# A hybrid encoder layer on one core: where in the program the weight sums of the down projection's Strassen groups are fetched

## The chip, the cores and the metric

The kernel runs on one core of a Trainium2 chip. The metric is the device time of one execution in microseconds (us), lower is better. The kernel before takes 2408.36 us, the median of three runs (2406.69 to 2409.8).

## The reference

One layer of a bidirectional encoder, in float32, on two requests of 256 tokens with 2048 features (512 tokens together):

```python
def encoder_layer(h, ...):
    xn = rmsnorm(h, norm_mix_w)
    proj = xn @ w_in                       # neighbourhood attention + gated delta net
    ...
    h = h + mixed                          # mixed = concat(...) @ w_out
    hn = rmsnorm(h, norm_ffn_w)
    return h + (jax.nn.silu(hn @ w_gate) * (hn @ w_up)) @ w_down
```

and a last rmsnorm. This document is about the last product, `(...) @ w_down`: 5632 hidden features to 2048, for 512 tokens.

## The kernel before, in words

**Arithmetic.** A float32 matrix is split into a high part (rounded to the fast float32 format by ScalarE, line 134) and a low part (the difference, VectorE, line 135). A product of two such matrices takes two or three matmuls. Every weight tile goes through this split on its way to TensorE.

**Stages.** In order of time: the input projection with the attention and delta-net heads (to about 900 us of the trace), the output projection, then gate and up (`scaled`, about 970 to 1840 us), then the down projection (1843 us to the end).

**A block.** Gate, up and most of down are computed by `block` (lines 969 to 1031). It is one step of a Strassen-like scheme with seven products instead of eight: two tiles of output features by two halves of the tokens, from four weight quarters `w11, w21, w12, w22`. A product (`product`, line 937) is a run of k-tiles, with two matmuls for each: 8 k-tiles in gate and up, 7 in the down projection (`GROUP = 7`). The seven products run on TensorE in this order, each with its weights and its PSUM tile:

1. `w11` (tile b11) into `ps_a`
2. `second = w12 + w22` into `ps_c`
3. `first = w11 + w12` into `ps_d`
4. `w21` (tile b21), into `ps_a` again
5. `first + b22` into `ps_b`
6. `w22` (tile b22), into `ps_d` again
7. `first + b21`, into `ps_c` again

The two sums `first` and `second` are made by DMA: a plain fetch of one quarter on SP's queue (lines 976 and 977), and then an accumulating fetch of the other on POOL's queue (`plus`, line 967, issued from lines 978 and 979), which can only be issued when the plain one has landed. The tiles b11, b21 and b22 are plain fetches on SP (lines 982 to 984). So a block has five plain loads and two accumulating ones. VectorE adds b22 (line 1015) and b21 (line 1027) to `first` in place.

Products are read out by VectorE and ScalarE (lines 949 to 953, 1003, 1009, 1020, 1021). The block's result is the tile `out`. It is created after the first product (line 996) and first written after the fourth, by ScalarE's copy of line 949 called from line 1013. At the end of the block it is added into the residual `hT` (line 1152).

**The down projection.** It runs in this order: a segment of 4 tiles done plainly (`down`), beside which the seven activation tiles of group 0 are combined (`combine`); group 0 (`down_group`, 8 blocks); another plain segment, beside which group 1 is combined; group 1 (8 blocks); two plain segments and the last norm. In the trace the blocks of group 0 start at 1881.30 us and end at 2069.85, those of group 1 go from 2113.41 to 2297.43. After blocks 2 and 4 of a group, `load_act` fetches one tile of the activations of the following plain segment, on POOL's queue (line 1119).

**Buffers.** All of these share one ring of five buffers, tag `ra` (`ring`, line 1101): the temporaries of `combine`, the two sums of a block, its `out`, and `load_act`'s tiles. The tiles b11, b21, b22 have a ring of three (tag `raw`), and the split weights have three high and three low parts. In gate and up, by contrast, `first` and `second` have buffers of their own, one set for gate and one for up.

**Order.** Matmuls are kept in the program's order. All other instructions are ordered on their engine when the program is compiled, by readiness and priority. The priority of an instruction is its place in the program, and `tc.high_priority(offset=n)` moves it n places ahead. `AHEAD` is 120. The splits of the weights have this offset, and the fetches at the head of a block 3 x 120 = 360. A block has about 140 instructions. SP and POOL issue their DMAs in the order so found, and an instruction that waits holds up those behind it on its queue. An instruction that is the first to write a tile needs a free buffer of the tile's ring.

Of the kernel before, what the change touches and what calls it, by code (L numbers as in the profile page):

```python
# [8 lines left out]
F32 = mybir.dt.float32  # L9
# [9 lines left out]
P = 128  # L19
# [5 lines left out]
L = 256  # L25
# [8 lines left out]
GROUP = 7  # L34
# [8 lines left out]
AHEAD = 120  # L43
# [26 lines left out]
def hybrid_encoder(ctx: ExitStack, tc: tile.TileContext, xT, w_in, w_ba, w_out, w_gate,  # L70
# [822 lines left out]
    XC = [hp.tile([P, 7, 2, L], F32R, tag=f"xc{k}", name="xc") for k in range(8)]  # L893
    ga_cm = tc.tile_pool(name="gA", bufs=1, side="left", reuse_waits="tile")
    gA = ga_cm.__enter__()
    acc = gA.tile([P, T], F32, tag="acc", name="ssq_acc2")
    A11, S3, S1, A12, S2, S4, A22 = range(7)
    for n, i in enumerate(pairs):
        j = i % 8
# [62 lines left out]
    def ahead():  # L962
        return tc.high_priority(offset=AHEAD)

    def plus(dst, src):

        nc.gpsimd.dma_start(dst, src, accum_op=ALU.add)

    def block(w4, new_w, xc, ix, p1_pool, new_out, opened=None):


        n = len(xc)
        w11, w21, w12, w22 = w4
        with tc.high_priority(offset=3 * AHEAD):
            first, second = new_w("first"), new_w("second")
            nc.sync.dma_start(second, w12)
            nc.sync.dma_start(first, w11)
            plus(second, w22)
            plus(first, w12)
            b11, b21, b22 = [wp.tile([P, 8, P], F32, tag="raw", bufs=3, name=nm)[:, :n]  # L980
                             for nm in ("b11", "b21", "b22")]
            nc.sync.dma_start(b11, w11)
            nc.sync.dma_start(b21, w21)
            nc.sync.dma_start(b22, w22)

        def bank(pool_, tag, nm):
            return pool_.tile([P, T], F32, tag=tag, name=nm).rearrange("p (a t) -> p a t", a=2)

        pa, pb = bank(pg, "g", "ps_a"), bank(pso, "o0", "ps_b")
        pc, pd = bank(psm, "s", "ps_c"), bank(pso, "o1", "ps_d")  # L990
        with ahead():
            w = w_split(b11)
        product(pa, w, xc, ix[A11], True)
        if opened:
            opened()
        fp, out = state["fp"], new_out()
        p1 = p1_pool.tile([P, L], F32, tag="p1", name="p1")
        plus_both(p1, None, pa)
        with ahead():
            w = w_split(second)  # L1000
        product(pc, w, xc, ix[S3], True)
        p7 = fp.tile([P, 2, L], F32, tag="p7", name="p7")
        nc.scalar.copy(p7, pc)
        with ahead():
            w = w_split(first)
        product(pd, w, xc, ix[S1], True)
        if opened:
            token_rstd2()
        tt(p7, pd, p7, ALU.subtract)
        with ahead():  # L1010
            w = w_split(b21)
        product(pa, w, xc, ix[A12], False, True)
        plus_both(out[:, 0], None, pa)
        with ahead():
            tt(first, first, b22, ALU.add)
            w = w_split(first)
        product(pb, w, xc, ix[S2], True, True)
        u2 = fp.tile([P, L], F32, tag="u2", name="u2")
        plus_both(u2, p1, pb)
        tt(out[:, 3], p7[:, 0], u2, ALU.subtract)  # L1020
        tt(out[:, 3], out[:, 3], p7[:, 1], ALU.add)
        with ahead():
            w = w_split(b22)
        product(pd, w, xc, ix[S4], False, True)
        plus_both(out[:, 2], u2, pd, ALU.subtract)
        with ahead():
            tt(first, first, b21, ALU.add)
            w = w_split(first)
        product(pc, w, xc, ix[A22], False, True)
        plus_both(out[:, 1], u2, pc)  # L1030
        return out
# [18 lines left out]

    def scaled(src, f, pool, new_out, opened=None):
        w4 = (src[f, 0], src[f, 1], src[f + 1, 0], src[f + 1, 1])
        out = block(w4, lambda nm: pool.tile([P, 8, P], F32, tag=nm, name="w_" + nm), XC,
                    range(7), gA, new_out, opened)
        a = out.rearrange("p (f b) t -> p f (b t)", f=2)
        tt(a, a, state["rstd2"][:, None, :].broadcast_to([P, 2, T]), ALU.mult)
        return out
# [37 lines left out]
    fq = ctx.enter_context(tc.tile_pool(name="fq", bufs=1, side="right", reuse_waits="tile"))  # L1095
    state["fp"] = fq
    XD = [hq.tile([P, 7, 2, L], F32R, tag=f"xd{k}", name="xd") for k in range(GROUP)]

    ix = (0, 3, 4, 1, 5, 6, 2)

    def ring(shape, nm):
        return fq.tile([P] + shape, F32, tag="ra", bufs=5, name=nm)
# [21 lines left out]
    def down(s, a, beside=None, first=False, residual=False):  # L1124

        for j in range(8):
# [14 lines left out]
            if residual:  # L1141
                plus(hcol(j), s_h2[2 * j:2 * j + 2].rearrange("i p t -> p i t"))

    def down_group(g, s):

        a = state["new_sA"]()
        for j in range(8):
            out = block([w_group[g, j, i] for i in range(4)],
                        lambda nm: ring([GROUP, P], "w_" + nm), XD, ix, fq,
                        lambda: ring([4, L], "out"))  # L1150
            h4 = hcol(j).rearrange("p i t -> p (i t)")
            tt(h4, h4, out.rearrange("p a t -> p (a t)"), ALU.add)
            if j in (2, 4):
                load_act(s, a, [j // 4])
        return a
# [148 lines left out]
```

## Time and profile before

| | |
|---|---|
| median of 3 runs | 2408.36 us (2406.69 to 2409.8) |
| the profiled execution | 2404.11 us, its span 2402.3 us, mean granted clock of TensorE 0.981 |
| TensorE busy | 2309.1 us, 96% of the span |
| VectorE busy | 1793.2 us, 75% |
| ScalarE busy | 1065.9 us, 44% |
| HBM | 163 GB/s over the span |
| group 0, blocks 0 to 7 | 1881.30 to 2069.85 us |
| group 1, blocks 0 to 7 | 2113.41 to 2297.43 us |

How to read the profile. PE is TensorE, PEld its weight loads, DVE VectorE, ACT ScalarE, POOL GpSimd, SP the sync engine. `L976` is line 976 of the kernel. `w_second<-in_w_group_dram` names what is written and what it is read from; buffer numbers are left out, so all blocks carry the same names. `SPq` and `POOL` with `DMA_DIRECT2D` are the issues of DMAs; the transfer itself ends some microseconds later. In a row of the timeline the columns are the start (us from the span's start), the length, engine, line, operation, tiles, and in brackets how long the engine had been idle and what ended that. In the rows of waits: who waited for whom, us in total, times, and the longest. A wait for several things is put down to what came last, so "DVE out" beside a POOL issue can stand for a DMA. In the view by windows each pair is the busy time and the count of one engine; PEclk is the granted clock as a share of the full one.

### The profile page before, as it was taken

To read this page: it belongs to the slowest core of one execution; us is meant where nothing else is said; L and a number is where in the kernel's file an instruction comes from. 1 tells how busy PE (TensorE), PEld (TensorE's weight loads), DVE (VectorE), ACT (ScalarE), POOL (GpSimd) and SP (SyncE) were. 2 spreads that over 40 slices of the span, in tenths; PEclk is the share of its full clock that TensorE was granted. 3 is DMA by queue.
4 is the path that set the end of the run, shared out by engine and by line. 5 is a ranking of instruction groups with operands and counts; after the bars stand their busy time and mean duration, and the time that the engine had idled before them with its cause. 6 is when DMAs were issued, how large, how long until landed. Compare 5 with 4: busy or idle time off the path is not lost.

```text
span 2402.3 us, 32408 instructions
## 1 busy us (share of the span) xinstructions
PE 2309.1 (96%) x12316; PEld 1940.6 (81%) x12316; DVE 1793.2 (75%) x2698; ACT 1065.9 (44%) x1626; POOL 246.3 (10%) x350
## 2 busy tenths in 40 slices
PE   9999999999999999999999999999999978988897
PEld 7887778887877788888888888888888767777687
DVE  7644899965656438988888888888888766866666
ACT  6786332343334216544444444444445423433335
POOL 2112100011000000101010101111000010000110
PEclk9999999999999999999999999999999989999899
DMA  5335322374335536777777677777774554554572
GB/s 198 132 110 157 104 101 93 105 173 143 130 116 177 170 123 222 206 203 202 203 198 200 189 215 194 209 203 195 199 184 156 142 162 125 183 152 135 163 184 89
DMA packets 113980, 393.19 MB, mean 164 GB/s; under 512 B 14336, under 2 KB 14800, under 8 KB 112544
## 3 DMA queue, kind: packets, MB, share of 16 engines
q1 hardware_dynamic: 78416, 275.56, 33.1%
q0 software_dynamic: 35408, 115.56, 22.4%
q8 instruction: 97, 1.59, 0.3%
q14 instruction: 59, 0.48, 0.1%
HBM read 355.59 MB, written 35.47 MB: 163 GB/s over the span
## 4 chain that ended last, share of the span: by engine, by line
PE 69%; DVE 15%; DMA 7%; ACT 5%; issue 4%; SPq 0%; POOL 0%; ACTq 0%; DVEq 0%; POOLq 0%
PE ps_g L82 21%; PE ps_c L82 13%; PE ps_d L82 12%; PE ps_a L82 11%; PE ps_b L82 6%; DMA w_second<-in_w_group_dram 5%; PE ps_s L82 5%; DVE w_lo L135 4%; ACT w_hi L134 2%; DVE prod L550 2%; DVE W L552 2%; PE ps_o L82 1%; DVE cacc L339 1%; DMA w_first<-in_w_group_dram 1%; ACT E L457 1%
## 5 line engine op out<-in xcount | busy, mean ns | idle before, releaser
L82 PE MATMUL ps_g<-xhi,w_hi 128*128 128x512 f32 x896 | 362.0, 404 | 2.1 <-DVE on L427 1.4
L82 PE MATMUL ps_g<-xhi,w_lo 128*128 128x512 f32 x896 | 350.8, 392 | 2.5 <-DVE w_lo L135 2.5
L82 PE MATMUL ps_g<-xlo,w_hi 128*128 128x512 f32 x896 | 350.4, 391 | 0.6 <-DVE xlo L243 0.4
L135 DVE TENSOR_TENSOR w_lo<-w_first,w_hi 128x1024 fp32r<-128x1024 f32 (+1 forms) x180 | 214.0, 1189 | 120.9 <-ACT w_hi L134 116.9
L134 ACT ACTIVATE w_hi<-w_raw 128x1024 fp32r<-128x1024 f32 x166 | 175.0, 1056 | 272.2 <-PE ps_g L82 213.3
L135 DVE TENSOR_TENSOR w_lo<-w_raw,w_hi 128x1024 fp32r<-128x1024 f32 x166 | 202.6, 1221 | 116.1 <-ACT w_hi L134 112.7
L134 ACT ACTIVATE w_hi<-w_first 128x1024 fp32r<-128x1024 f32 (+1 forms) x180 | 185.8, 1032 | 231.2 <-PE ps_c L82 105.7
L134 ACT ACTIVATE w_hi<-b 128x1024 fp32r<-128x1024 f32 (+1 forms) x180 | 185.6, 1031 | 218.9 <-issue 123.1
L82 PE MATMUL ps_a<-xc,w_hi 128*128 128x512 f32 x704 | 251.7, 397 | 1.0
L82 PE MATMUL ps_d<-xc,w_hi 128*128 128x512 f32 x704 | 249.7, 394 | 0.0
L82 PE MATMUL ps_c<-xc,w_hi 128*128 128x512 f32 x704 | 249.7, 394 | 0.0
L135 DVE TENSOR_TENSOR w_lo<-b,w_hi 128x1024 fp32r<-128x1024 f32 (+1 forms) x180 | 213.3, 1185 | 11.6 <-ACT w_hi L134 4.6
L82 PEld LDWEIGHTS ps_g<-xhi,w_hi 128*128 128x128 f32 x896 | 168.7, 188 | 39.7 <-issue 6.6
L82 PEld LDWEIGHTS ps_g<-xhi,w_lo 128*128 128x128 f32 x896 | 168.5, 188 | 39.9 <-DVE w_lo L135 3.9
L82 PE MATMUL ps_a<-xc,w_lo 128*128 128x256 f32 x704 | 197.0, 280 | 0.0
L82 PE MATMUL ps_c<-xc,w_lo 128*128 128x256 f32 x704 | 196.9, 280 | 0.0
L82 PE MATMUL ps_d<-xc,w_lo 128*128 128x256 f32 x704 | 196.9, 280 | 0.0
L82 PEld LDWEIGHTS ps_g<-xlo,w_hi 128*128 128x128 f32 x896 | 168.8, 188 | 34.6 <-DVE xlo L243 1.8
L82 PEld LDWEIGHTS ps_a<-xc,w_hi 128*128 128x128 f32 x704 | 131.9, 187 | 36.6 <-issue 6.3
L82 PE MATMUL ps_c<-xd,w_hi 128*128 128x512 f32 x224 | 105.0, 491 | 53.9 <-ACT w_hi L134 53.9
L82 PEld LDWEIGHTS ps_c<-xc,w_hi 128*128 128x128 f32 x704 | 131.9, 187 | 30.7
L82 PEld LDWEIGHTS ps_d<-xc,w_hi 128*128 128x128 f32 x704 | 131.9, 187 | 30.7
(358 smaller groups left out, 4752.6 us busy)
## 6 DMA issues: line engine op xcount, KB each, us to landing
w_raw<-in_w_in_dram SPq DMA_DIRECT2D x110, 512.0 KB, 3.3
b<-in_w_gate_dram SPq DMA_DIRECT2D x66, 512.0 KB, 4.2
b<-in_w_up_dram SPq DMA_DIRECT2D x66, 512.0 KB, 5.5
b<-in_w_group_dram SPq DMA_DIRECT2D x48, 448.0 KB, 4.9
w_raw<-in_w_out_dram SPq DMA_DIRECT2D x32, 512.0 KB, 3.4
w_raw<-in_w_down_dram SPq DMA_DIRECT2D x32, 512.0 KB, 4.3
w_second<-in_w_gate_dram SPq DMA_DIRECT2D x22, 512.0 KB, 8.1
w_first<-in_w_gate_dram SPq DMA_DIRECT2D x22, 512.0 KB, 5.8
```

Source lines behind the costliest of these rows:

```text
L82: pin(nc.tensor.matmul(*a, **k))
L134: act(out=hi, in_=src, func=AF.Copy)
L135: tt(lo, src, r32(hi), ALU.subtract)
L339: stt(a3[:, :, lo:hi], x3[:, :, lo + o:hi + o], cw[:, ct, j:j + 1], a3[:, :, lo:hi], ALU.mult, ALU.add)
L457: pin(act(out=E[half[0], s, s:], in_=G[half[0], s:], func=AF.Exp, bias=NG[half[0], s:s + 1]))
L550: tt(pv, W[:, s0:s1, s0:c], kkq[:, c, 0, None, s0:c].broadcast_to([P, n, j]), ALU.mult)
L552: nc.vector.tensor_reduce(W[:, s0:s1, c], pv, AX.X, ALU.add)
```

## The change

The fetch of the two sums becomes a function of its own, `weight_sums`, with the same four DMAs in the same order and the same priority offset. `block` takes the two sums ready made. In gate and up, `scaled` calls `weight_sums` directly ahead of `block`, so that nothing moves there. In `down_group` the sums of block 0 are fetched ahead of the loop, and those of block j+1 inside block j: `block` calls `new_out()` after its first product, which creates `out` and then calls `group_sums(g, j + 1)`. In the program the fetches of block j+1 thus stand behind the first product of block j, ahead of the instructions that evict it, instead of at the head of block j+1.

```diff
-    def block(w4, new_w, xc, ix, p1_pool, new_out, opened=None):
-
-
-        n = len(xc)
+    def weight_sums(w4, new_w):
+
         w11, w21, w12, w22 = w4
         with tc.high_priority(offset=3 * AHEAD):
             first, second = new_w("first"), new_w("second")
...
             nc.sync.dma_start(first, w11)
             plus(second, w22)
             plus(first, w12)
+        return first, second
+
+    def block(w4, sums, xc, ix, p1_pool, new_out, opened=None):
+
+        n = len(xc)
+        first, second = sums
+        w11, w21, w12, w22 = w4
+        with tc.high_priority(offset=3 * AHEAD):
             b11, b21, b22 = [wp.tile([P, 8, P], F32, tag="raw", bufs=3, name=nm)[:, :n]
                              for nm in ("b11", "b21", "b22")]
             nc.sync.dma_start(b11, w11)
...
+    def group_sums(g, j):
+        return weight_sums([w_group[g, j, i] for i in range(4)],
+                           lambda nm: ring([GROUP, P], "w_" + nm))
+
     def down_group(g, s):
 
         a = state["new_sA"]()
+        sums = [group_sums(g, 0)]
+
+        def new_out():
+            out = ring([4, L], "out")
+            if j < 7:
+                sums.append(group_sums(g, j + 1))
+            return out
+
         for j in range(8):
-            out = block([w_group[g, j, i] for i in range(4)],
-                        lambda nm: ring([GROUP, P], "w_" + nm), XD, ix, fq,
-                        lambda: ring([4, L], "out"))
+            out = block([w_group[g, j, i] for i in range(4)], sums[j], XD, ix, fq, new_out)
             h4 = hcol(j).rearrange("p i t -> p (i t)")
             tt(h4, h4, out.rearrange("p a t -> p (a t)"), ALU.add)
```

More of the change, by code (lines that the diff above doesn't have):

```diff
@@ L1052, in scaled @@
         w4 = (src[f, 0], src[f, 1], src[f + 1, 0], src[f + 1, 1])
-        out = block(w4, lambda nm: pool.tile([P, 8, P], F32, tag=nm, name="w_" + nm), XC,
-                    range(7), gA, new_out, opened)
+        sums = weight_sums(w4, lambda nm: pool.tile([P, 8, P], F32, tag=nm, name="w_" + nm))
+        out = block(w4, sums, XC, range(7), gA, new_out, opened)
         a = out.rearrange("p (f b) t -> p f (b t)", f=2)
```

## The prediction

> **What bounds the kernel now.** I read the page first: the busy shares, the 40 slices, and the chain that ended last.
>
> ```profile
> PE 2309.1 (96%) x12316; PEld 1940.6 (81%) x12316; DVE 1793.2 (75%) x2698; ACT 1065.9 (44%) x1626; POOL 246.3 (10%) x350
> PE   9999999999999999999999999999999978988897
> PEclk9999999999999999999999999999999989999899
> PE ps_g L82 21%; PE ps_c L82 13%; PE ps_d L82 12%; PE ps_a L82 11%; PE ps_b L82 6%; DMA w_second<-in_w_group_dram 5%; PE ps_s L82 5%; DVE w_lo L135 4%; ACT w_hi L134 2%; DVE prod L550 2%; DVE W L552 2%; PE ps_o L82 1%; DVE cacc L339 1%; DMA w_first<-in_w_group_dram 1%; ACT E L457 1%
> ```
>
> TensorE is full in 31 slices, and then come the slices of the down projection's two groups with 7 and 8. The chain has one large DMA in it, the fetch of a weight sum of the groups: 5% of 2402 us is 120 us. So I asked for the sums by stretch: blocks 1 to 7 of group 0, the same of group 1, and, to compare, eight blocks of the gate and up projections, which run the same seven products over eight k-tiles instead of seven. Columns: length, then busy us (and count) of PE, weight loads, DVE, ACT and POOL, granted clock, DMA share, GB/s.
>
> ```profile
> 1902.56:2069.85 167.29, 136.63 (x688) 115.05 (x687) 108.91 (x151) 57.66 (x75) 13.38 (x17) 0.89 0.53 145
> 2131.61:2297.43 165.82, 137.16 (x688) 115.71 (x687) 108.98 (x150) 56.88 (x73) 13.43 (x18) 0.90 0.54 148
> 1301.01:1458.83 157.82, 157.60 (x903) 137.64 (x902) 135.03 (x174) 71.75 (x85) 15.98 (x20) 1.00 0.71 195
> ```
>
> A gate block takes 157.82/8 = 19.73 us with TensorE never idle and the clock at 1.00. The larger tiles should cost 8/7 of a group block, so a group block's own matmul time is 19.73 x 14/16 = 17.26 us (each k-tile is two matmuls). But a group block takes 167.29/7 = 23.90 and 165.82/7 = 23.69 us. TensorE is idle 30.66 + 28.66 = 59.3 us there, and its clock is 0.89 and 0.90. What ends the idle time (the waits of this stage: us, times, longest), and one block boundary in order of time:
>
> ```profile
> ACT w_hi L134 <- DMA w_second<-in_w_group_dram: 128.7, 15, 10.6
> PE ps_c L82 <- ACT w_hi L134: 53.9, 15, 5.2
> ...
> 1965.87 0.33 SPq L983 DMA_DIRECT2D b<-in_w_group_dram  x1
> 1966.25 0.42 SPq L976 DMA_DIRECT2D w_second<-in_w_group_dram  x1
> 1966.72 0.42 SPq L977 DMA_DIRECT2D w_first<-in_w_group_dram  x1
> 1967.24 0.38 SPq L984 DMA_DIRECT2D b<-in_w_group_dram  x1
> ...
> 1966.30 0.37 ACT L949 COPY out<-ps_a 128x256 f32<-128x256 f32 x1 [1.59 <-PE ps_a L82]
> ...
> 1972.16 0.85 POOL L967 DMA_DIRECT2D w_second<-in_w_group_dram  x1 [22.26 <-DVE out L952]
> 1973.36 0.86 POOL L967 DMA_DIRECT2D w_first<-in_w_group_dram  x1 [0.34 <-issue]
> ...
> 1973.52 0.40 PE L82 MATMUL ps_a<-xd,w_hi 128*128 128x512 f32 x1
> ...
> 1979.28 0.95 ACT L134 ACTIVATE w_hi<-w_second 128x896 fp32r<-128x896 f32 x1 [9.63 <-DMA w_second<-in_w_group_dram]
> 1980.29 0.80 PE L82 MATMUL ps_c<-xd,w_hi 128*128 128x512 f32 x1 [4.13 <-ACT w_hi L134]
> 1982.07 0.95 ACT L134 ACTIVATE w_hi<-w_first 128x896 fp32r<-128x896 f32 x1 [1.84 <-DMA w_first<-in_w_group_dram]
> ```
>
> A block starts on TensorE at 1973.52. Its second sum was fetched at 1966.25, added to by POOL's DMA at 1972.16, and split by ACT at 1979.28: 13.0 us from fetch to use. A product lasts 17.26/7 = 2.47 us, so the second product could begin at 1976.0; it begins at 1980.29. That is 4.3 us late, in 15 of 16 blocks.
>
> **Why the fetch is late.** The sums share a ring of five buffers with `out`. The fetch has a priority of 360 places ahead, yet it leaves at the moment when `out` of the block before is first written: 1966.25 against 1966.30. It is the same one block into the group, where the ring is nearly empty (the last temporary of the seven combinations is written at 1880.01, its last reader starts at 1881.56, and only the two sums of block 0 are live):
>
> ```profile
> 1880.01 0.42 DVE L1110 TENSOR_TENSOR cmd<-raw_a,cmd 128x256 f32<-128x256 f32 x1
> 1881.56 1.23 DVE L135 TENSOR_TENSOR xd<-cmd,xd 128x1024 fp32r<-128x1024 f32 x1 [1.13 <-ACT xd L134]
> ...
> 1895.33 0.37 SPq L976 DMA_DIRECT2D w_second<-in_w_group_dram  x1
> ...
> 1895.34 0.37 ACT L949 COPY out<-ps_a 128x256 f32<-128x256 f32 x1 [1.60 <-PE ps_a L82]
> 1896.95 1.09 DVE L135 TENSOR_TENSOR w_lo<-w_first,w_hi 128x896 fp32r<-128x896 f32 x1 [0.75 <-ACT w_hi L134]
> ```
>
> I read this so: buffers of a ring are given out in the order in which the program first writes the tiles, not by priority and not by which is free. `out` is first written after the fourth product (line 1013), and the next block's sums come behind it. Creation order is not what counts: `first` is created before `second`, but the rows have L976 (`second`) ahead of L977 (`first`), as the program writes them.
>
> **The change, part by part.** No instruction is added or removed. The two plain fetches (SP) and the two accumulating ones (POOL) of block j+1 are now written in the program behind block j's first product and ahead of `out`'s first write. By the reading above the ring's order becomes: sums of j+1, then `out` of j. So the sums of j+1 can leave as soon as `out` of block j-1 has its buffer and one is free. Second: `out` of j-1 is written 1973.52 - 1966.30 = 7.2 us before block j starts, which is 24.5 us before block j+1 does. It needs 13.0 us and is wanted 1.5 us into the block (one product less ACT's 0.95): some 13 us to spare, where it now lacks 4.3. First: with `out` of j-1, the sums of j and `first` of j-1 in the ring, its buffer comes when `first` of j-1 is split for the last time; that split ends at 1896.95 + 1.09 = 1898.04, 4.5 us before the next block (1902.56), so it leaves 21.8 us ahead of block j+1. From 1966.72 to 1982.07 it takes 15.4 us, and it is wanted 4 us into the block: 10 us to spare.
>
> The queues passed (issues of the whole run: KB each, median us to landing):
>
> ```profile
> b<-in_w_group_dram SPq DMA_DIRECT2D x48, 448.0 KB, 4.9
> w_second<-in_w_group_dram SPq DMA_DIRECT2D x16, 448.0 KB, 4.2
> w_second<-in_w_group_dram POOLq DMA_DIRECT2D x16, 448.0 KB, 7.2
> w_first<-in_w_up_dram POOLq DMA_DIRECT2D x22, 512.0 KB, 8.8
> ```
>
> On SP the sums now stand a block ahead of where they were, among the same five loads of 448 KB per block; SP's issues take 0.33 to 0.42 us (above). Their buffer is free by then, so they hold up b21 (1965.87) or b22 by one issue. On POOL they pass the two loads of the segment's activations per group, which are not due for blocks. Nothing new waits.
>
> The gain: blocks 1 to 7 fall to 17.26 us each. Group 0: 167.29 - 7 x 17.26 = 46.5 us; group 1: 165.82 - 120.8 = 45.0 us; together 91.5 us. Of this 59.3 is recorded idle time, and 32.2 is matmuls that run slowly behind it. The clock of 0.89 and 0.90 in the rows above says why: it drops at each wait. The Trainium skill ("TensorE: Matmul & The Clock Gate", Part 1) states that after an idle window of about 3.4 us the array runs at half clock for about as long again; that would be an estimated 1.7 us for each of 14 waits, 24 us, and a gain of 83 us instead of 91.5. The trace agrees in kind (0.89 to 0.90 against 1.00) and has 2.3 us for each.
>
> What comes late next, and its price. (1) DVE. It is the cover's thinnest part:
>
> ```profile
> 1973.52:1997.85 24.33, 19.87 (x101) 16.58 (x99) 16.12 (x22) 8.69 (x11) 2.83 (x4) 0.86 0.56 155
> 1997.85:2021.78 23.93, 19.12 (x100) 16.24 (x99) 15.07 (x21) 7.67 (x10) 1.12 (x3) 0.93 0.51 130
> 2113.41:2131.61 18.20, 17.57 (x99) 14.97 (x98) 13.42 (x19) 7.56 (x10) 0.80 (x1) 1.00 0.46 132
> ```
>
> DVE is busy 15.07 us per block, 16.12 with a load of activations, against 17.26: 87% and 93%. The gate blocks hide 135.03/157.82 = 86% without a trace of a stall. I bound it by 0 (the gate) and 0.7 us per block (10 us in 14 blocks), and take 0.2 us: 3 us, nearest to the gate. (2) Block 0 of each group. Its own sums come just in time (the last row is block 0 of group 1: 18.20 us, 0.63 idle), and now those of block 1 are fetched right behind them. Two plain loads of 448 KB at the gate's 195 GB/s are 2 x 2.35 = 4.7 us of traffic. It costs nothing if the sums of block 0 are ahead in every queue, and up to 4.7 us per group if they share: I take 1.5 each, 3 us. (3) DMA bandwidth: a group moves 148 GB/s x 23.69/17.26 = 203 GB/s afterwards, beside 195 at a share of 0.71 in the gate; no price, but it is in bound (1).
>
> **Sum.** 91.5 - 3 - 3 = 85.5 us. The profiled execution took 2404.1 us (span 2402.3 and 1.8 around it), so 2318.6; the median of the three runs is 4.3 above it, which gives 2322.9, say 2323. For the best case, the first matmuls of two products of a block that follow each other:
>
> ```profile
> 2014.50 0.39 PE L82 MATMUL ps_b<-xd,w_hi 128*128 128x512 f32 x1
> 2016.93 0.39 PE L82 MATMUL ps_d<-xd,w_hi 128*128 128x512 f32 x1
> ```
>
> No residue and products of 2016.93 - 2014.50 = 2.43 us (17.0 per block): 167.29 + 165.82 - 238 = 95, so 2313. Worst of this case: 91.5 - 10 - 9.4 = 72: 2336.
>
> **Rivals.**
> *A, the change doesn't move the fetch.* If buffers go in order of creation, `out` is still created ahead of the sums, and they leave as now, at L949: 2408. For it: in the diff `ring([4, L], "out")` does stand first. Against it: L976 ahead of L977, above. 0.07.
> *B, the loads of the block's own weights become the late ones.* If the early sums stand ahead of b21 on SP and wait for a buffer that the add into `hT` frees, b21 comes late (the add's row, in the block boundary above):
>
> ```profile
> 1974.64 1.22 DVE L1152 TENSOR_TENSOR hT<-hT,out 128x1024 f32<-128x1024 f32 x1
> ```
>
> The add ends at 1975.86, 2.3 us after the block's start. b21 leaves at start + 2.8, lands a median 4.9 us later, and its split takes ACT and DVE some 2.1 us (0.95 + 1.09): 9.8, where the fourth product is due at 3 x 2.47 = 7.4. That is a stall of 2.4 us in each of 14 blocks, 34 us: 2357. Against it: `second`'s own buffer is free early in every block. 0.10.
> *C, slower.* The same queue, with a longer wait: SP serves in order, so a sum that waits for its buffer holds b21, b22 and b11 behind it. b21 now leaves 7.65 us before the block's start, and by B's sum it can leave as late as 0.4 us behind it (7.4 - 4.9 - 2.1): 8 us to spare. Beyond that each us is a us per block. It outweighs the present 23.8 - 17.26 = 6.5 us from a delay of 14.5 us on; at 15.5 us it gives 14 x 1 = +14: 2422. For it: the ring of five is full (first of j-1, both sums of j, `out`, one sum of j+1) for a part of each block, and accumulating DMAs land in up to 8.8 us in the up projection. Against it: every buffer in question is freed by a split or an add within a block's last 5 us or the next one's first 3. 0.03.
>
> **Chances.** The forecast 0.80, A 0.07, B 0.10, C 0.03. The range takes the forecast's own ends, 1.5 us of scatter of the three runs below, and half of the way to B: 2311 to 2345. A measurement of this kernel tells about 0.2% (5 us) from no change: faster by more than that 0.90, within it 0.07, slower 0.03.
>
> **What would show it.** Right: L976 leaves 24 us or more ahead of its block's `ps_a`, not 7; "ACT w_hi <- DMA w_second" and "PE ps_c <- ACT w_hi" are gone from the waits of the groups but for block 0; blocks 1 to 7 take 17.0 to 17.9 us, clock 1.00, DVE at 86 to 93% of them. Wrong: L976 beside L949 again (A); idle time ahead of `ps_a`'s second product that L134 of `b` ends (B, C); block 0 over 23 us. A stall that stays with `first` instead of `second` would mean that the ring's fifth buffer is the limit.

## The result, and the profile after

| | before | after |
|---|---|---|
| median | 2406.69 us (2404.65 to 2409.8, 5 runs) | 2314.91 us (2313.67 to 2318.97, 5 runs) |
| profiled execution, span | 2404.11, 2402.3 us | 2313.67, 2311.9 us |
| blocks 1 to 7 of group 0, of group 1 | 167.29, 165.82 us | 118.90, 118.90 us |
| block 0 of group 0, of group 1 | 21.26, 18.20 us | 23.02, 19.51 us |

The ratio is 0.9619, with a 95% interval of 0.9605 to 0.9633: 91.8 us less by the medians, where 85.5 were forecast. First the page of the kernel after: busy shares, the 40 slices, the granted clock, the chain that ended last.

```profile
PE 2274.4 (98%) x12316; PEld 1922.5 (83%) x12316; DVE 1791.7 (77%) x2698; ACT 1066.0 (46%) x1626; POOL 246.3 (11%) x350
PE   9999999999999999999999999999999999999997
PEclk9999999999999999999999999999999999999998
PE ps_g L82 23%; PE ps_c L82 14%; PE ps_d L82 14%; PE ps_a L82 14%; PE ps_b L82 7%; PE ps_s L82 4%; DVE w_lo L135 2%; DVE prod L550 2%; DVE W L552 2%; PE ps_o L82 1%; ACT w_hi L134 1%; DVE cacc L339 1%; DMA w_second<-in_w_group_dram 1%; DMA w_raw<-in_w_down_dram 1%; ACT E L457 1%
```

The slices of 7 and 8 in the groups are full, and the fetch of `w_second` has gone from 5% of the chain to 1%. The same stretches by windows, blocks 1 to 7 of each group and then block 0 of each (columns as before: length, PE, weight loads, DVE, ACT, POOL, granted clock, DMA share, GB/s):

```profile
1902.28:2021.18 118.90, 118.90 (x688) 104.94 (x687) 107.17 (x150) 56.63 (x74) 12.53 (x16) 1.00 0.72 188
2084.25:2203.15 118.90, 118.90 (x688) 103.95 (x687) 107.57 (x150) 55.80 (x72) 12.48 (x16) 1.00 0.73 192
...
1879.26:1902.28 23.02, 20.36 (x100) 17.29 (x99) 15.18 (x20) 9.62 (x13) 1.84 (x3) 0.85 0.78 186
2064.74:2084.25 19.51, 17.57 (x99) 14.86 (x98) 13.67 (x20) 8.51 (x11) 0.86 (x1) 1.00 0.74 174
```

In blocks 1 to 7 TensorE is busy for the whole of 118.90 us, 16.99 us a block, at a granted clock of 1.00. DVE is busy 107.17/118.90 = 90% of it. The waits of this stage that were the largest are left with two cases, the two blocks 0:

```profile
ACT w_hi L134 <- DMA w_second<-in_w_group_dram: 6.3, 2, 5.7
...
PE ps_c L82 <- ACT w_hi L134: 3.3, 2, 2.0
```

Now SP's queue and the copy into `out` in block 1, in order of time. After's lines are 974 and 975 for the fetches of `second` and `first`, 988 to 990 for b11, b21, b22:

```profile
1910.54 0.33 SPq L989 DMA_DIRECT2D b<-in_w_group_dram  x1
1912.10 0.33 SPq L990 DMA_DIRECT2D b<-in_w_group_dram  x1
1912.52 0.38 SPq L974 DMA_DIRECT2D w_second<-in_w_group_dram  x1
1912.97 0.35 ACT L949 COPY out<-ps_a 128x256 f32<-128x256 f32 x1
...
1933.90 0.96 ACT L134 ACTIVATE w_hi<-w_second 128x896 fp32r<-128x896 f32 x1 [0.47 <-PE ps_d L82]
```

The fetch still stands close to a copy into `out`, but it is no longer the sum of the next block. The fetch of 1912.52 is the fourth of the group, for block 3; that block starts at 1902.28 + 2 x 16.99 = 1936.26, 23.7 us later. ACT's split of this sum at 1933.90 waited for a product (`PE ps_d`) and not for a DMA. For blocks 2 to 7 of both groups the lead is 22.0 to 24.1 us, where it was 7.3 at the boundary shown in the prediction.

The end of the kernel, from the last block to the end of the span, before and after:

```profile
2297.43:2402.30 104.87, 92.37 (x590) 83.79 (x588) 66.05 (x113) 47.57 (x83) 9.70 (x8) 0.96 0.53 141
```

```profile
2203.15:2311.90 108.75, 94.13 (x590) 85.43 (x588) 66.34 (x114) 47.56 (x83) 9.68 (x8) 0.93 0.52 137
```

It got 3.9 us longer, which nothing in the prediction provides for. And group 0 starts 2.0 us earlier (1879.26 against 1881.30), upstream of everything that was changed; in the other kernels of this document that start scatters from 1876.2 to 1881.3. The difference of the spans in parts: 48.4 + 46.9 us from blocks 1 to 7, less 1.8 + 1.3 in the blocks 0, less 3.9 at the end, plus 2.0 upstream: 90.3 of the 90.4 us between the spans.

### The profile page after: what moved, and what is told of

It is laid out like the page before. It is cut to its first block, busy times and chain, and to the rows that moved or that the text cites. A ratio compares the mean times of both kernels' runs of the same rounds, so it can differ in the third digit from the quotient of the medians.

```text
span 2311.9 us, 32451 instructions
## 1 busy us (share of the span) xinstructions
PE 2274.4 (98%) x12316; PEld 1922.5 (83%) x12316; DVE 1791.7 (77%) x2698; ACT 1066.0 (46%) x1626; POOL 246.3 (11%) x350
## 4 chain that ended last, share of the span: by engine, by line
PE 78%; DVE 12%; ACT 4%; DMA 3%; issue 3%; POOL 0%; SPq 0%; DVEq 0%; ACTq 0%; POOLq 0%
PE ps_g L82 23%; PE ps_c L82 14%; PE ps_d L82 14%; PE ps_a L82 14%; PE ps_b L82 7%; PE ps_s L82 4%; DVE w_lo L135 2%; DVE prod L550 2%; DVE W L552 2%; PE ps_o L82 1%; ACT w_hi L134 1%; DVE cacc L339 1%; DMA w_second<-in_w_group_dram 1%; DMA w_raw<-in_w_down_dram 1%; ACT E L457 1%
## 5 line engine op out<-in xcount | busy, mean ns | idle before, releaser
L82 PEld LDWEIGHTS ps_a<-xc,w_lo 128*128 128x128 f32 x704 | 133.1, 189 | 0.3 <-issue 0.2
```

Source lines behind the costliest of these rows:

```text
L82: pin(nc.tensor.matmul(*a, **k))
```

## The experiments

Theory T is the prediction's: the order in which the tiles of the ring are first written in the program decides where the fetches can stand, so "ahead of `out`'s first write" is what counts. In the recorded texts T is each time this theory with what it expects of that run, and R1 to R8 are rivals. The first rival, R1, is that the mere number of places ahead does it.

**More priority, same place** (kernel before):

```diff
-        with tc.high_priority(offset=3 * AHEAD):
+        with tc.high_priority(offset=6 * AHEAD):
```

> The kernel before with one number changed: the sums' priority offset is 720 places ahead instead of 360; their place in the program stays (head of their block, behind `out`'s first write). Theory T (the ring's buffers are given out in the program order of the tiles' first writes): the fetch still waits for the preceding `out`'s first write, so w_second's fetch still leaves beside ACT L949 some 7 us ahead of its block, blocks 1 to 7 keep 23.7 to 23.9 us, time 2400 to 2410 us. Rival R1 (the change won because the fetch stands more places ahead in the queue): the fetch leaves some 24 us ahead, blocks of 17.0 us, time near 2315 us.

2407.05 us, ratio 1.0 (0.999 to 1.0011). At one block boundary SP's queue is as it was, and the copy into `out` starts at 1963.52:

```profile
1963.13 0.33 SPq L983 DMA_DIRECT2D b<-in_w_group_dram  x1
1963.51 0.42 SPq L976 DMA_DIRECT2D w_second<-in_w_group_dram  x1
1963.99 0.42 SPq L977 DMA_DIRECT2D w_first<-in_w_group_dram  x1
```

Twice the priority moves nothing: the fetch already asked for more than it could get.

**One statement's difference** (kernel after; `then` is the fetch of block j+1's sums):

```diff
         product(pa, w, xc, ix[A12], False, True)
+        if then:          # first kernel: ahead
+            then()
         plus_both(out[:, 0], None, pa)
+        if then:          # second kernel: behind, instead
+            then()
```

> The changed kernel with the fetches of block j+1's sums moved down by three products, to the place directly ahead of the statement that first writes `out` of block j (behind the fourth product). Theory T: the sums are still ahead of `out` in the ring's order, so nothing changes: blocks 1 to 7 of 17.0 us, time 2310 to 2322 us. Rival R1 (places ahead in the program are what counts): about 3 of 7 products' lead are lost, some 7 us, so a lead of about 15 to 17 us against 13.0 us needed for `second`: close to the edge, time 2320 to 2350 us.

> As the run that has the fetches directly ahead of the statement that first writes `out`, but directly behind it: the two differ by the order of two statements and nothing else. Theory T: `out` of block j is now ahead of the sums of j+1 in the ring's order, the fetch leaves beside ACT L949 again some 7 us ahead of its block, the wait of 4.3 us for each of 14 blocks comes back: 2395 to 2410 us. Rival R1 (place in the program, not the ring's order): as its neighbour, within 5 us of it.

Ahead: 2313.77 us, ratio 0.9615 (0.9599 to 0.9631). Behind: 2410.59 us, ratio 1.0012 (0.9999 to 1.0026). Each as expected by T. The two kernels differ in the order of two statements, and that order is worth the whole change. R1 falls: three products further down in the program cost nothing, one statement costs everything. The windows of the first (blocks 1 to 7 of each group), and one boundary of the second:

```profile
1901.94:2020.84 118.90, 118.90 (x688) 103.96 (x687) 107.19 (x150) 56.64 (x74) 12.53 (x16) 1.00 0.73 189
2085.94:2204.84 118.90, 118.90 (x688) 103.97 (x687) 107.04 (x149) 55.81 (x72) 12.29 (x16) 1.00 0.73 188
```

```profile
1959.56 0.33 SPq L990 DMA_DIRECT2D b<-in_w_group_dram  x1
...
1959.98 0.38 SPq L974 DMA_DIRECT2D w_second<-in_w_group_dram  x1
...
1961.17 0.35 ACT L949 COPY out<-ps_a 128x256 f32<-128x256 f32 x1
```

The second fence holds a correction. The late fetch leaves 1.2 us before the copy into `out`. So it does not wait for that copy on the chip. It leaves 0.42 us behind b22's issue on SP, as it left 0.38 us behind b21's in the kernel before (1966.25 against 1965.87) and in the first experiment (1963.51 against 1963.13). In the kernel before it is b21 that waits; here are SP's waits in blocks 1 to 7 of group 0:

```profile
SPq L983 <- DVE w_lo L135: 94.4, 6, 16.6
...
SPq L983 <- DMA b<-in_w_group_dram: 16.4, 6, 3.4
```

L983 is b21, which waits for one of the three buffers of the tag `raw`. The split that ends its wait at 1965.87 is that of b22 of the block before, which ends at 1964.75 + 1.09 = 1965.84:

```profile
1964.75 1.09 DVE L135 TENSOR_TENSOR w_lo<-b,w_hi 128x896 fp32r<-128x896 f32 x1 [0.22 <-ACT w_hi L134]
```

In the four kernels with both sums late (before, more priority, behind `out`, and the filled wait below) the fetch of `second` leaves 0.40 to 0.46 us behind the end of this split in all blocks 1 to 7 but one (1.07 us), whether b21 or b22 stands between. The order of the program's statements decides where the fetch stands in SP's queue; in the queue it goes when this split has freed a buffer of the tag `raw`. No row shows a wait of L976 itself.

**`out` out of the ring** (kernel before, the fetches where they were; the ring has four buffers and `out` one, the same memory):

```diff
-        return fq.tile([P] + shape, F32, tag="ra", bufs=5, name=nm)
+        return fq.tile([P] + shape, F32, tag="ra", bufs=4, name=nm)
...
-                        lambda: ring([4, L], "out"))
+                        lambda: fq.tile([P, 4, L], F32, tag="out", name="out"))
```

> The kernel before, the fetches at their old place at the head of their own block, but `out` has a buffer of its own and the ring `ra` four buffers instead of five (the same memory). Theory T: the sums no longer stand behind `out` in a common order, so they leave as soon as a buffer of the four is free: lead of 13 us or more, blocks 1 to 7 near 17.0 to 18 us, time 2312 to 2340 us. Rival R1 (the place in the program): no change, 2400 to 2410 us. Rival R3 (the ring's count of buffers, not its order, held the fetch back): no better than before, since the sums have fewer buffers than before.

2318.8 us, ratio 0.9631 (0.9615 to 0.9647). Blocks 1 to 7 of each group:

```profile
1902.59:2023.07 120.48, 119.84 (x689) 104.97 (x687) 108.04 (x154) 58.21 (x77) 12.19 (x16) 1.00 0.66 180
2085.83:2206.94 121.11, 120.14 (x688) 104.84 (x687) 106.29 (x149) 55.40 (x72) 11.66 (x15) 1.00 0.67 179
```

No fetch was moved in the program, and nearly the whole gain is there: the fetches of `second` for blocks 1 to 7 of group 0 now leave 25 to 34 us ahead of their blocks. R1 falls again: it was the shared order, and not the place. R3 falls less clearly by this run alone, since four buffers now serve two tiles of a block where five served three. It falls by the pair before, which has five buffers in both kernels. With the one statement's difference this settles the cause, as far as the program's order goes.

**The wait filled** (kernel before; 36 small matmuls with an unused result between the first and the second product of each group block):

```diff
+        if n == GROUP:
+            warm = sm_tile()
+            for _ in range(FILL):
+                mm(warm[:, :2 * P], idle[:, :P], idle, start=True, stop=True)
         product(pc, w, xc, ix[S3], True)
```

> The kernel before, with 36 small bf16 matmuls (128x256, into a spare bank, result unused) between the first and the second product of each group block; the fetches stay late. It separates the two parts of the gain, the wait itself (59.3 us of idle time in blocks 1 to 7) and the slow matmuls behind it (2.3 us per wait by the prediction, 32 us). Theory T (the clock drops because TensorE is idle): with the wait filled the clock stays near 1.00 and the wait's length stays as it is, so 20 to 34 us of the gain come without moving a fetch: 2374 to 2387 us. Rival R5 (the products behind the wait are slow because their splits come late, not by the clock): no gain, 2400 to 2415 us.

2403.27 us, ratio 0.9982 (0.9969 to 0.9995), that is 1.2 to 7.5 us less, of the 18 to 31 expected. T's expectation is missed. Blocks 1 to 7 of both groups by windows (PE's busy time holds the filler too):

```profile
1901.07:2067.44 166.37, 155.56 (x940) 131.28 (x939) 108.01 (x150) 56.11 (x75) 13.47 (x18) 0.98 0.54 144
2131.87:2296.60 164.73, 154.96 (x941) 131.41 (x939) 108.33 (x150) 55.39 (x73) 13.60 (x18) 0.98 0.55 146
```

The filler did its work: the granted clock is 0.98 where it was 0.89 and 0.90. It takes 3.9 us and is not what holds up the second product, which starts later than the filler's end in all but two of the 14 blocks. And the blocks still take 166.37/7 = 23.77 and 23.53 us. What took the place of the slow matmuls is in the waits of that stretch, in the kernel before and here (this kernel's lines are one higher):

```profile
ACT w_hi L134 <- DMA w_first<-in_w_group_dram: 9.2, 6, 2.3
```

```profile
ACT w_hi L135 <- DMA w_second<-in_w_group_dram: 138.8, 15, 11.5
...
ACT w_hi L135 <- DMA w_first<-in_w_group_dram: 23.1, 11, 3.4
```

`first` is late 11 times now instead of 6, and `second` no less than before (128.7 us, 15 times). The rows of one block show a loop:

```profile
1957.00 0.95 ACT L135 ACTIVATE w_hi<-w_first 128x896 fp32r<-128x896 f32 x1 [2.58 <-DMA w_first<-in_w_group_dram]
...
1964.92 1.08 DVE L136 TENSOR_TENSOR w_lo<-b,w_hi 128x896 fp32r<-128x896 f32 x1
...
1966.03 0.33 SPq L985 DMA_DIRECT2D b<-in_w_group_dram  x1
1966.41 0.42 SPq L977 DMA_DIRECT2D w_second<-in_w_group_dram  x1
...
1981.36 0.95 ACT L135 ACTIVATE w_hi<-w_first 128x896 fp32r<-128x896 f32 x1 [2.99 <-DMA w_first<-in_w_group_dram]
```

`first` lands and is split (1957.00). ACT and DVE then split b21, `first + b22` and b22. The end of b22's split frees the buffer for which SP's queue waits, and behind it stand the next block's sums (1966.41), whose landing lets the next split of `first` begin (1981.36). No step of it has slack. The split of `first` begins when its transfer lands. From there to the end of b22's split ACT and DVE work in a fixed order and wait for each other and for no product; from the split of `first` to the fetch pass 9.4 us in each of the blocks here, whatever TensorE does (8.3 to 9.6 us, 9.0 on the mean, in the kernel before). The fetch leaves 0.41 us behind the end of b22's split. From the fetch to the next split of `first`, transfers with POOL's issue between them, pass 14.4 us on the mean here and 14.8 before. So the loop sets the period, 23.8 us here and 23.7 before in blocks 2 to 7. In the kernel before it goes mostly through `second`, whose landing ends ACT's wait 15 times, with the split of `first` 2 to 3 us behind. Faster matmuls hardly shorten such a loop; TensorE waits longer instead.

The edit is not pure. In the compiled kernel b22 stands ahead of the sums on SP, `first + b21` stands ahead of b22's split on DVE, and the loop's first part is 0.4 us longer than before. The price of the slow clock alone is thus not measured by this run; what it shows is that the clock does not set the period.

**Half of the change**: only one of the two sums ahead of `out`'s first write, the other directly behind it.

```diff
         product(pa, w, xc, ix[A12], False, True)
+        if then:
+            then(0)       # fetches one of the sums of block j+1
         plus_both(out[:, 0], None, pa)
+        if then:
+            then(1)       # fetches the other
```

> One half of the change: of block j+1's two sums only `second` is fetched ahead of `out`'s first write, `first` stays directly behind it. Theory T with the loop that the run with the filled wait points to (a late sum is fetched when `out` of the block before is first written, 7.2 us before its block, and the block's own later products wait for it, so that the period of a block is the loop from one write of `out` to the next): w_second's waits are gone, w_first still leaves beside ACT L949. Alone on the queues it is split some 12 us after its fetch (w_second took 11.7 to 13.9 us in the kernel before), and the third product, wanted 4.9 us into the block, starts 1 to 3 us late: period 18 to 20 us, time 2328 to 2365 us. Rival R6 (only `second` was ever late): as the changed kernel, 2312 to 2320.

> The other half: only `first` is fetched ahead of `out`'s first write, `second` directly behind it. Theory T: w_second still leaves beside ACT L949, and the second product waits for it as in the kernel before (3 to 4.5 us); the loop through `second` (12 us to its split, the split, and then three products with the slow clock behind the wait) stays at 22 to 23.8 us: 2375 to 2407 us, most of the gain is missing. Rival R7 (the two sums share the fetch's delay by their traffic, so half the traffic is half the delay): near the middle, 2345 to 2370 us.

`second` alone: 2372.95 us, ratio 0.9851 (0.9834 to 0.9868), 36 us of the 92. `first` alone: 2410.48 us, ratio 1.0001 (0.9989 to 1.0013), nothing. The halves don't add up to the whole, which fits the loop: one late sum is enough to keep it. R6 and R7 fall. But the first of the two runs was mis-sized by me (2328 to 2365 expected). Its waits in blocks 1 to 7 of both groups and SP's queue at one place:

```profile
ACT w_hi L134 <- DMA w_first<-in_w_group_dram: 85.7, 14, 8.8
```

```profile
1979.67 0.33 SPq L994 DMA_DIRECT2D b<-in_w_group_dram  x1
1980.05 0.43 SPq L977 DMA_DIRECT2D w_first<-in_w_group_dram  x1
1980.79 0.33 SPq L975 DMA_DIRECT2D w_second<-in_w_group_dram  x1
```

In all 14 blocks ACT waits for `first`, which leaves behind b22, which waits for its buffer; the early `second` of the block after leaves right behind it. Its way from the fetch to the split was sized rightly all the same: 12.0 us on the mean, as expected. Too small was what follows the wait: from the start of product 3 to that of product 4 pass 3.6 to 6.0 us instead of 2.4, and a block takes 20.7 and 21.0 us in the two groups, where 18 to 20 were expected.

**Block 0** (kernel after; the sums of block 0 of each group are fetched ahead of the seventh combination instead of behind it, and in a second kernel ahead of the sixth):

```diff
             if beside is not None and j < GROUP:
                 combine(beside + j, j)
+                if j == 5:            # second kernel: j == 4
+                    state["sums"] = group_sums(beside // GROUP, 0)
...
-        sums = [group_sums(g, 0)]
+        sums = [state["sums"]]
```

> The changed kernel, and the sums of block 0 of each group are also fetched earlier in the program: in the plain segment ahead of the group, behind the sixth of the seven combinations and ahead of the seventh, so that they stand ahead of the seventh combination's two temporaries in the ring. Theory T (the ring's order sets when a sum leaves): w_second of block 0 leaves some 5 us earlier or more, the wait of the second product of block 0 (2.7 us idle in group 0, with the slow matmuls behind it 23.0 us instead of 17.0; 19.5 in group 1) shrinks or goes: 17 to 20 us for block 0, 4 to 8.5 us off the changed kernel's 2314.9, so 2306 to 2311. Rival R4 (block 0 is late because of DMA traffic, share 0.78 there, or because the seventh combination itself is late): block 0 keeps 19.5 to 23 us, time 2312 to 2317.

> As the run with block 0's sums ahead of the seventh combination, one combination earlier (behind the fifth). There w_second of group 0 left at 1870.49, 0.4 us behind the issue of b11, which stands ahead of it on SP and waits for a buffer of the tag `raw`; block 0 of group 0 still took 21.9 us, of group 1 17.5. Here the two sums stand ahead of b11 (group 0) and of b22 (group 1). Theory T: they leave as soon as the fourth combination's temporaries are free, some 5 us earlier, block 0 takes 17.0 to 18.5 us in both groups, 3 to 5 us off that run's 2309.1: 2303 to 2307 us. Rival R8: the sums hold two of five buffers while two combinations are still to be made, the sixth and seventh wait for theirs, and the first or later products of block 0 wait for the last `xd` instead: block 0 above 21 us, or the plain segment ahead of it grows, 2309 to 2325 us.

The first: 2309.08 us, ratio 0.9597 (0.9582 to 0.9611), the best of all by the median. Its interval meets that of the kernel after (0.9605 to 0.9633), so by the times alone the 3 to 6 us are likely, not shown. The second: 2313.86 us, 0.9616 (0.9599 to 0.9633). Block 0 of both groups, first kernel and second kernel:

```profile
1878.81:1900.71 21.90, 19.13 (x99) 16.25 (x98) 16.36 (x23) 10.05 (x14) 3.01 (x4) 0.92 0.86 211
2063.18:2080.67 17.49, 17.49 (x99) 14.90 (x98) 17.14 (x25) 8.52 (x11) 1.72 (x2) 1.00 0.78 204
```

```profile
1878.81:1898.99 20.18, 18.32 (x100) 14.97 (x99) 16.99 (x25) 10.30 (x15) 1.71 (x2) 1.00 0.74 202
2063.72:2082.67 18.95, 17.60 (x99) 14.96 (x98) 18.61 (x27) 8.95 (x12) 1.70 (x2) 1.00 0.70 182
```

23.02 + 19.51 us became 21.90 + 17.49, and then 20.18 + 18.95: a gain of 3.1 us, and 3.4 from the earlier place, so hardly more. In the first kernel T's 17 to 20 us for block 0 hold in group 1 and R4's 19.5 to 23 in group 0. In the second T's time (2303 to 2307) is missed, and R8's mechanism shows in group 0, though its block 0 stays below the 21 us that R8 named. The sums do leave 5.3 us earlier (1865.24 against 1870.49), but now the last `xd` is late, and the first two products wait for it:

```profile
PE ps_c L82 <- DVE xd L135: 0.9, 1, 0.9
...
PE ps_a L82 <- DVE xd L135: 0.8, 1, 0.8
```

Of the 4.2 us between the two profiled executions (2308.11 and 2312.34), 2.3 are no doing of the edit: blocks 1 to 7 of group 0 take 118.89 us in the first and 121.21 in the second, both without idle time (see the last section).

**The tail** (the residual's eight accumulating loads out of the last plain segment: into the middle one; the same with block 0's sums early; or one per block of group 1 with block 0's sums early):

```diff
-    down(MID_SEG, a, GROUP)
+    down(MID_SEG, a, GROUP, residual=True)
...
-    down(LAST_SEGS[0], a, residual=True)
+    down(LAST_SEGS[0], a)
```

> The changed kernel, and the eight accumulating loads of the residual into `hT` stand in the middle plain segment instead of the last one. Theory T (the longer tail of the changed kernel's profile, 108.75 us against 104.87 from the end of group 1 on, has nothing to do with the change: the last plain segment runs the DMA engines at a share of 0.98 to 1.03 in its second half in both kernels, and the first wait of the final stage is for what lands there): the share there falls to 0.7 or less, the stage behind it takes 28 to 29 us instead of 29.0 to 31.9, time 2 to 4 us below the changed kernel's, 2311 to 2313. Rival: the final stage waits for its own weights whatever else is loaded: no difference, 2313 to 2317; or block 0 of group 1 becomes late behind the loads that now stand ahead of it: up to 5 us slower.

> The changed kernel with both edits, block 0's sums ahead of the seventh combination and the residual's loads in the middle segment. If both theories hold the gains add: 6 to 12 us below the changed kernel, 2303 to 2309 us; if the residual's loads in the middle segment delay block 0's sums on POOL, less than the first edit alone.

> The changed kernel with block 0's sums ahead of the seventh combination, and the residual's eight accumulating loads one per block of group 1 (behind each block's add into `hT`) instead of in the last plain segment. In the middle segment those loads stood ahead of block 0's sums and cost what they saved (block 0 of group 1 took 26.9 and 23.0 us). Theory: in the group the DMA engines have room (share 0.73) and the sums are due a block ahead, so nothing waits; the final stage keeps the 27.35 us without idle time that it had with the residual moved: 2 to 4 us below the kernel that moves the sums alone (2309.1), 2304 to 2308 us. Rival: the loads wait on POOL for each block's add and hold the accumulating loads of the next sums behind them: blocks of group 1 grow, 2309 to 2325 us.

Middle segment: 2316.6 us, ratio 0.9628 (0.9609 to 0.9646). With block 0's sums: 2314.05 us, 0.9615 (0.9601 to 0.963). In the group: 2311.65 us, 0.9593 (0.9579 to 0.9607). In the first of the three, by windows, block 0 of group 1 (what the edit cost) and the stage behind the segment from which the loads were taken, the first request's half of the last segment (what was hoped for):

```profile
2064.38:2091.27 26.89, 19.56 (x99) 16.07 (x98) 14.35 (x21) 8.48 (x11) 6.86 (x7) 0.87 1.06 245
...
2253.74:2281.09 27.35, 27.35 (x229) 27.34 (x228) 15.59 (x36) 16.51 (x36) 0.00 (x0) 1.00 0.01 1
```

That stage takes 29.01 us in the kernel before and 31.92 after, here 27.35 with TensorE busy throughout. That much of the theory holds, but its time (2311 to 2313) is missed, and the second rival, a late block 0, is met. Block 0 of group 1, 19.51 us in the kernel after, takes 26.89: its second product waits 6.4 us for the split of `second`, and the DMA engines are at a share of 1.06 there. The load that was taken from one crowded place seems to crowd another; that it is the DMA engines and not the order on POOL's queue was not isolated. With block 0's sums early, block 0 of group 1 still takes 23.04 us, and the gains don't add (2303 to 2309 expected).

Moved into group 1's blocks the load mostly finds room (share 0.83) and the stage keeps its 27.35 us, yet the expected 2304 to 2308 us are missed, and the time is that of the kernel with the sums alone, within the intervals. Blocks 1 to 7 of both groups in that kernel:

```profile
1902.66:2023.84 121.18, 121.18 (x688) 105.15 (x687) 107.39 (x149) 56.58 (x74) 12.52 (x16) 1.00 0.71 184
2084.92:2206.94 122.02, 120.53 (x689) 104.93 (x688) 107.08 (x149) 55.57 (x72) 21.30 (x23) 1.00 0.83 214
```

Group 0, which has none of these loads, is 2.3 us longer than in the kernel after, with no idle time and the same granted clock. That is the difference of the last section and not the edit's. Group 1 has a pause of 1.5 us: in one block ACT waits 4.4 us for a tile of `load_act`, whose fetch stands behind one of these loads on POOL, and the splits of the weights wait behind it. That is near to what the rival said. Whether the edit is worth 2 or 3 us stays open.

## Why the prediction was right, point by point

**The bound.** Right: TensorE at 98%, the wait for `second` gone but for the two blocks 0, the slices full.

**The reading of the ring.** Right in what it was used for: the order of first writes in the program decides. Priority does not (ratio 1.0), nor the place in the program as such (0.9631 with nothing moved, and the pair of 0.9615 and 1.0012). Rival A ("the change doesn't move the fetch") fell with the result. But one step was wrongly told. The fetch was said to leave "at the moment when `out` of the block before is first written". The two times agree to 0.05 us in the kernel before, and that was a coincidence: with the fetch behind `out` in the changed kernel it leaves 1.2 us before the copy. On the chip it stands behind b21, or b22, on SP, and leaves when b22 of the block before has been split. How the compiling step turns the ring's order into that place in the queue was not taken apart further. And no run gave `raw` a fourth buffer, which would tell how much of the wait is b21's alone.

**The lead.** "24 us or more" is 22.0 to 24.1: 2 us less, out of some 13 us to spare.

**The gain of blocks 1 to 7.** Forecast 91.5 less 3 for VectorE, 88.5; measured 48.4 + 46.9 = 95.3. Two terms were mis-sized. The product was taken as 2.47 us from the gate blocks, and is 2.43, which stood in the text as the best case: 14 x (17.26 - 16.99) = 3.8 us. About a third of that was the window: it holds 903 matmuls, seven more than eight blocks have (8 x 112), and the 56 products from 1301.01 on end at 1458.07, 157.06 us or 17.18 us for a group block. The rest are slower products and short pauses in it (last section). That the groups of the profiled execution ran at the shorter product throughout is luck, as the last section shows. And VectorE's residue of 3 us is 0: at 90% it hid everything, as it did at 86% in the gate.

**The two parts of the gain.** The sum was right, its split says less than it seemed to. It counted 59.3 us of waits and 32.2 us of slow matmuls behind them. The slow matmuls are real: from the start of product 2 to that of product 3 pass 4.6 to 5.4 us in the 14 blocks of the kernel before, with no recorded wait over 0.6 us in it, where 2.43 are enough. And the low clock goes when the wait is filled (0.98 against 0.89 and 0.90). But filling it brought 1.2 to 7.5 us, since the loop, and not TensorE, sets the block's period. The two parts can't be gained one without the other. The Trainium skill ("TensorE: Matmul & The Clock Gate", Part 1) was weighed in the prediction for the length of a slow stretch; by its estimate the gain would have been 83 us. The measured 95.3 us of blocks 1 to 7 decides between neither that and the 2.3 us per wait, since the whole loop went and the product was mis-sized too.

**Block 0.** Forecast +3, measured 1.8 + 1.3 = 3.1. That is a hit by luck in a scattered quantity. The sign "block 0 over 23 us", which the prediction named for being wrong, came: 23.02 us in group 0, and 23.45 with the sums directly ahead of `out`. It stands for a cost of block 0 larger than forecast in that group, with less in the other. Both blocks 0 together take 39.5 us in the kernel before (21.26 + 18.20), 40.8 in the run with more priority and 40.6 in the one with the sums behind `out`. They take 42.5 in the kernel after, 45.0 with the sums directly ahead of `out`, and 43.7 with `out` out of the ring. So early sums cost block 0 some 2 to 5 us. That they do it by sharing the DMA engines was not isolated.

**The rest of the miss.** The profiled execution was forecast at 2318.6 us and took 2313.67: 4.9 us less. That is +6.8 us of gain in blocks 1 to 7, -0.1 in block 0, +2.0 upstream and -3.9 at the end. The end isn't the change's doing. In the run with more priority, whose groups are those of before, it is just as long:

```profile
2298.47:2406.85 108.38, 94.14 (x590) 85.45 (x588) 66.32 (x114) 47.58 (x83) 9.70 (x8) 0.93 0.53 137
```

In three kernels with late sums the tail takes 104.9, 108.4 and 107.8 us, in three with early ones 108.8, 106.5 and 105.8. It scatters by 3 us or more in both. Of the 3.9 us, 2.9 lie in the stage that the loads into `hT` hold up (29.01 and 31.92 us). I read the scatter as these loads landing sooner or later; without them that stage took 27.35 us in two runs. The other 3.1 us lie in the median: 4.3 us above the profiled execution in the runs of before, 1.2 after.

**Rivals B and C.** TensorE has no idle time in the 14 blocks, so no product waited for b21 or b22; nothing came of either. (The 8.8 us that C took for the longest landing is the median of its row.)

## What to carry to other kernels

When tiles of one ring are written by different engines at different places of the program, the order of their first writes is a schedule of its own: look there, not at the priority, when a prefetch with room to spare leaves late. Moving one statement, or giving one tile its own buffer, was worth 4%. A wait that recurs in each step with a fixed period may be a loop, and the trace can tell: follow one tile from its landing to the next fetch and to the next landing, and see whether each step begins when the one before it ends. The parts of a loop can't be priced one by one: here half of the change brought 39% or nothing, and faster matmuls, which are hardly part of the loop, brought almost nothing. So before an account such as "idle plus slow" is used for a smaller edit, ask what sets the period.

## What the runs showed of the hardware

Products of the same matmuls at the same granted clock come in two lengths: 118.90 and 121.18 us for the same 688 recorded matmuls of blocks 1 to 7, both without idle time and with a clock of 1.00 in the rows. That is 1.9%, or 2.43 and 2.47 us for a product. Both lengths stand in the trace of every kernel here, and within the kernel before they change from block to block. In gate and up, with eight k-tiles, the same two are 2.83 and 2.77 us, by the starts of products that follow each other (kernel before):

```profile
1315.14 0.40 PE L82 MATMUL ps_a<-xc,w_hi 128*128 128x512 f32 x1
...
1317.97 0.40 PE L82 MATMUL ps_b<-xc,w_hi 128*128 128x512 f32 x1
...
1354.52 0.39 PE L82 MATMUL ps_a<-xc,w_hi 128*128 128x512 f32 x1
...
1357.30 0.39 PE L82 MATMUL ps_b<-xc,w_hi 128*128 128x512 f32 x1
```

The length is kept as long as product follows product. In the groups of all 14 traces, some 1540 boundaries between products, it changes only where a product begins late, with one exception (in the run with `out` out of the ring). In the kernels with late sums, which pause in every block, it is drawn anew there; in those with early sums a group can keep one length throughout. What sets the length at a pause stays open. The gate window from which 17.26 us per block was worked out holds both lengths, and a pause at each new pair of blocks (2.85 to 3.01 us for the products there). An account from a stretch of matmuls is thus good to about 2%, whatever the granted clock says, and so is a comparison of two executions.
